# Row mean of 64 MB: a first part of one row per partition in place of sixteen

## The chip, the cores and the metric

The kernel runs on one core of a Trainium2 chip. The metric is the device time of one execution in microseconds (us), given as the median of several runs. The engines that matter here are VectorE (DVE in the profile), ScalarE (ACT), GpSimd (POOL), SyncE (SP, which here only issues DMAs), and the 16 DMA engines that move data between the chip's memory (HBM) and the on-chip memory of 128 partitions (SBUF).

## The reference

```python
def setup_inputs():
    batch, seq, dim = 32, 512, 1024
    return {"x": np.random.randn(batch, seq, dim).astype(np.float32), "divisor": float(dim)}

def reference(x, divisor):
    return (np.sum(x, axis=-1) / divisor).astype(np.float32)
```

There are 32 x 512 = 16,384 rows of 1,024 float32 values, 4 KB a row and 67.1 MB in all. Each row is summed and the sum is divided by 1,024. The result is 64 KB.

## The kernel before

Each of the 128 partitions gets 128 rows (J = 128). The rows are split into three parts, each with its own access pattern into the input.

- The *first* part is F = 16 rows per partition: partition p reads rows 16p to 16p+15 of the first 2,048 rows, so from partition to partition the address goes on by 64 KB. It is read by two loads, of 2 and 14 rows per partition.
- The *main* part is M = 96 rows and the *last* part L = 16 rows per partition. Together they are W = 112 consecutive rows of a partition, so from partition to partition the address goes on by 448 KB. The main part is read by seven loads: five of 14 rows, one of 14 and one of 12.
- The last part is read by loads of 9, 4 and 2 rows, and its sixteenth row in two halves, `pa` and `pb`.

A load of n rows is one DMA of 128 pieces, one per partition, and a piece is n x 4 KB long. All loads are issued from SP in program order (L182), on one queue. The nine loads of the first and main part and the load of 9 rows use a pool of three buffers (`bulk`), 14 rows each. So a load must wait until the reduce of the load three before it has ended. The loads of 4 and 2 rows and the two halves have buffers of their own.

VectorE sums the rows of a bulk load with one instruction (L205). In the last two bulk loads of the main part, ScalarE takes 4 and 5 of the rows (L186); in the lists `first`, `main` and `last` the second number of a pair says how many. POOL multiplies the sums of a part by 1/1024 (L207): `res0` for the first part, `res` for the main part. In the last part, VectorE (L192) and ScalarE sum and scale row by row into `fin`.

Three stores write the result, all from SP: `o_first` (L223) and `o_main` (L224) are placed behind the last loads in program order, `o_last` (L228) stands at the very end. Their pieces are one per partition: 64 B, 384 B and 64 B; in the output, the main and last pieces of neighbouring partitions are 448 B apart.

Three functions change the finished program. `start_loads_at_once` moves the first loads, those without a wait, ahead of the opening barrier; there are three. `latest_wait_first` reorders the waits of an instruction. `close_while_storing` moves the last store into the closing sequence, so that the engines close while it is in flight; POOL there waits for the landings of the first two stores, and SP's last instruction for the landing of the third.

Of the kernel before, what the change touches and what calls it, by code (L numbers as in the profile page):

```python
# [9 lines left out]
F32 = mybir.dt.float32  # L10
# [115 lines left out]
@with_exitstack  # L126
def kernel(
    ctx: ExitStack,
    tc: tile.TileContext,
    x: bass.AP,  # L130
    divisor: float,
    out: bass.AP,
):
    nc = tc.nc
    landed = nc.alloc_semaphore("landed")
    nc.at_finalize(start_loads_at_once)
    nc.at_finalize(latest_wait_first)
    nc.at_finalize(lambda nc: close_while_storing(nc, landed))
    xf = x.flatten_outer_dims()
    N, D = xf.shape  # L140
    P = nc.NUM_PARTITIONS
    scale = 1.0 / float(divisor)
    J = N // P
    assert J * P == N


    F, L = 16, 16
    M = J - F - L
    W = M + L
    x_first = bass.AP(tensor=x.tensor, offset=0, ap=[[F * D, P], [D, F], [1, D]])  # L150
    x_main = bass.AP(tensor=x.tensor, offset=P * F * D, ap=[[W * D, P], [D, M], [1, D]])
    x_last = bass.AP(tensor=x.tensor, offset=P * F * D + M * D, ap=[[W * D, P], [D, L], [1, D]])
    o_first = bass.AP(tensor=out.tensor, offset=0, ap=[[F, P], [1, F]])
    o_main = bass.AP(tensor=out.tensor, offset=P * F, ap=[[W, P], [1, M]])
    o_last = bass.AP(tensor=out.tensor, offset=P * F + M, ap=[[W, P], [1, L]])


    first = [(2, 0), (14, 0)]
    main = [(14, 0)] * 5 + [(14, 4), (12, 5)]
    last = [(9, 4), (4, 2), (2, 1)]  # L160
    assert sum(n for n, _ in first) == F
    assert sum(n for n, _ in main) == M and sum(n for n, _ in last) == L - 1

    pad = ctx.enter_context(tc.tile_pool(name="pad", bufs=1))
    pad.tile([P, 224], F32, name="pad")
    bulk = ctx.enter_context(tc.tile_pool(name="bulk", bufs=3))
    one = ctx.enter_context(tc.tile_pool(name="one", bufs=1))
    psum = ctx.enter_context(tc.tile_pool(name="junk", bufs=4, space=bass.MemoryType.PSUM))


    c = 512
    t4 = one.tile([P, 4, D], F32, name="t4")
    t2 = one.tile([P, 2, D], F32, name="t2")
    pa = one.tile([P, 768], F32, name="pa")[:, :c]
    pb = one.tile([P, D - c + 16], F32, name="pb")[:, : D - c + 2]
    res0 = one.tile([P, F], F32, name="res0")
    res = one.tile([P, M], F32, name="res")
    fin = one.tile([P, L], F32, name="fin")
    nc.gpsimd.memset(pb[:, D - c :], 0.0)  # L179

    def load(dst, src):
        tc.keep_in_program_order(nc.sync.dma_start(out=dst, in_=src))  # L182

    def act_sum(dst, src, by=1.0):
        junk = psum.tile([P, D], F32, name="junk")
        nc.scalar.activation(junk, src, COPY, scale=by, accum_out=dst)  # L186

    def dve_mean(dst, src, by=scale):


        h = src.shape[-1] // 2
        nc.vector.tensor_tensor_reduce(  # L192
            out=src[:, :h], in0=src[:, :h], in1=src[:, h:], scale=by, scalar=0.0,
            op0=ADD, op1=ADD, accum_out=dst,
        )

    for loads, src, dst in ((first, x_first, res0), (main, x_main, res)):
        j = 0
        for rows, on_act in loads:
            t = bulk.tile([P, 14, D], F32, name="t")  # L200
            load(t[:, :rows, :], src[:, j : j + rows, :])
            d = rows - on_act
            for i in range(d, rows):
                act_sum(dst[:, j + i : j + i + 1], t[:, i, :])
            nc.vector.reduce_sum(out=dst[:, j : j + d], in_=t[:, :d, :], axis=AX)  # L205
            j += rows
        nc.gpsimd.tensor_scalar_mul(out=dst, in0=dst, scalar1=scale)  # L207
    j = 0
    for rows, on_act in last:
        t = bulk.tile([P, 14, D], F32, name="t")[:, :rows, :] if rows > 4 else t4 if rows == 4 else t2  # L210
        load(t, x_last[:, j : j + rows, :])
        d = rows - on_act
        for i in range(rows):
            if i < d:
                dve_mean(fin[:, j + i : j + i + 1], t[:, i, :])
            else:
                act_sum(fin[:, j + i : j + i + 1], t[:, i, :], by=scale)
        j += rows
    load(pa, x_last[:, j, :c])
    load(pb[:, : D - c], x_last[:, j, c:])  # L220


    tc.keep_in_program_order(nc.sync.dma_start(out=o_first, in_=res0))  # L223
    tc.keep_in_program_order(nc.sync.dma_start(out=o_main, in_=res))  # L224

    dve_mean(pb[:, D - c : D - c + 1], pa, by=1.0)
    dve_mean(fin[:, j:], pb)
    tc.keep_in_program_order(nc.sync.dma_start(out=o_last, in_=fin))  # L228
# [35 lines left out]
```

## Time and profile before

| | |
|---|---|
| median of 3 runs | 160.81 us (160.39 to 160.96) |
| span of the profiled execution | 159.0 us (the page gives no other time of it; the median is 1.8 us longer) |
| DMA, bytes moved, mean rate | 67.18 MB, 422 GB/s over the span |
| VectorE busy | 117.2 us (74%), of which the bulk reduces 111.2 us |
| ScalarE busy | 18.5 us (12%) |
| POOL busy | 1.0 us (1%) |
| landing of the first load (2 rows) | 4.63 us after the span's start |
| a reduce of 14 rows | 15.09 us |
| last store, issue to landing | 1.4 us |

The span begins with the issue of the first load and ends with the landing of the last store. An engine's share of busy time is an average over the span; what a change in one stage is worth has to be read from that stage, by the wait that ends last there. In the slices of the page each digit is the busy share of a fortieth of the span in tenths. A group's line gives what was waited for, the total of the waits in us, their number, and the longest.

### The profile page before, as it was taken

Reading aid. Unit: us, or ns where it says so; the run is one execution under the profiler, and the core shown is the slowest. Engines: PE = TensorE matmul, PEld = TensorE weight load, DVE = VectorE, ACT = ScalarE, POOL = GpSimd, SP = SyncE. Lnnn points to the kernel's source line nnn. Section 1 sums busy time; section 2 is a strip of 40 time slices with the busy share of each in tenths; the row PEclk is TensorE's granted clock in tenths of the full one; section 3 lists DMA queues with packets and bytes.
Section 4 is the critical chain, followed back from the end, with each engine's and each line's share of the span. In section 5 each row is a group of like instructions: output and inputs, shape, how many; then the busy total and the mean of one; then the engine's idle time right before and its main releaser. Section 6 shows DMA issues by size and latency. Waiting matters only on the chain.

```text
span 159.0 us, 148 instructions
## 1 busy us (share of the span) xinstructions
DVE 117.2 (74%) x29; ACT 18.5 (12%) x33; POOL 1.0 (1%) x7
## 2 busy tenths in 40 slices
DVE  0500059995999599978999599959995996395643
ACT  3000000000000000000000000000000900390684
POOL 0000000000000000000000000000000000001000
DMA  7999999959999999699999999699999999999894
GB/s 278 447 462 462 462 462 462 462 260 433 462 462 462 462 462 462 303 390 462 462 462 462 462 462 404 303 447 462 462 462 429 396 396 408 482 445 445 350 420 169
DMA packets 2448, 67.18 MB, mean 422 GB/s; under 512 B 656, under 2 KB 656, under 8 KB 912
## 3 DMA queue, kind: packets, MB, share of 16 engines
q1 hardware_dynamic: 2448, 67.18, 98.3%
HBM read 67.11 MB, written 0.07 MB: 422 GB/s over the span
## 4 chain that ended last, share of the span: by engine, by line
DMA 77%; DVE 21%; SPq 1%; issue 0%; DVEq 0%
DMA t<-in_x_dram 56%; DMA pb<-in_x_dram 21%; DVE res L205 20%; SPq L182 1%; DVE pb L192 0%; DVEq L259 0%
## 5 line engine op out<-in xcount | busy, mean ns | idle before, releaser
L205 DVE TENSOR_REDUCE res<-t 128x14 f32<-128x14336 f32 (+3 forms) x9 | 111.2, 12360 | 34.0 <-DMA t<-in_x_dram 34.0
L186 ACT ACTIVATE junk<-t 128x1024 f32<-128x1024 f32 x16 | 16.2, 1013 | 136.8 <-DMA t<-in_x_dram 136.8
L192 DVE CUSTOM_DVE_ANT_0 t<-t 128x512 f32<-128x512 f32 x8 | 5.1, 688 | 6.1 <-DMA t<-in_x_dram 6.1
L186 ACT ACTIVATION_READ_ACCUMULATOR junk<-t 128x1 f32 x16 | 3.0, 186 | 0.0
L207 POOL TENSOR_SCALAR res<-res 128x16 f32<-128x16 f32 (+1 forms) x2 | 0.7, 352 | 143.3 <-DVE res L205 143.3
L186 ACT ACT_TABLE_LOAD x1 | 1.3, 1283 | 1.7 <-PEq L245 1.7
L192 DVE DVE_READ_ACCUMULATOR2_ANT fin<- 128x1 f32 x9 | 0.7, 82 | 0.0
L192 DVE CUSTOM_DVE_ANT_0 pb<-pb 128x257 f32<-128x257 f32 x1 | 0.4, 428 | 0.2 <-DMA pb<-in_x_dram 0.2
L192 DVE CUSTOM_DVE_ANT_0 pa<-pa 128x256 f32<-128x256 f32 x1 | 0.4, 426 | 0.0
L179 POOL MEMSET pb<- 128x2 f32 x1 | 0.1, 99 | 1.3 <-POOLq L245 1.3
L245 POOL MEMSET const-bfloat16-1.0<- 128x1 bf16 x1 | 0.1, 101 | 0.0
L245 POOL MEMSET const-uint8-127<- 128x1 uint8 x1 | 0.1, 101 | 0.0
L245 POOL MEMSET const-float32-0.0<- 128x1 f32 x1 | 0.1, 98 | 0.2 <-issue 0.2
L245 POOL MEMSET const-float32-1.0<- 128x1 f32 x1 | 0.1, 98 | 0.0
L192 DVE DVE_READ_ACCUMULATOR2_ANT pb<- 128x1 f32 x1 | 0.1, 84 | 0.0
## 6 DMA issues: line engine op xcount, KB each, us to landing
t<-in_x_dram SPq DMA_DIRECT2D x7, 7168.0 KB, 35.6
t<-in_x_dram SPq DMA_DIRECT2D x1, 6144.0 KB, 33.3
t<-in_x_dram SPq DMA_DIRECT2D x1, 4608.0 KB, 27.2
t<-in_x_dram SPq DMA_DIRECT2D x2, 1024.0 KB, 19.2
t<-in_x_dram SPq DMA_DIRECT2D x1, 2048.0 KB, 31.7
pa<-in_x_dram SPq DMA_DIRECT2D x1, 256.0 KB, 33.8
pb<-in_x_dram SPq DMA_DIRECT2D x1, 256.0 KB, 33.9
out_dram<-res SPq DMA_DIRECT2D x1, 48.0 KB, 11.6
```

The costliest lines, as they stand in the source:

```text
L179: nc.gpsimd.memset(pb[:, D - c :], 0.0)
L182: tc.keep_in_program_order(nc.sync.dma_start(out=dst, in_=src))
L186: nc.scalar.activation(junk, src, COPY, scale=by, accum_out=dst)
L192: nc.vector.tensor_tensor_reduce(out=src[:, :h], in0=src[:, :h], in1=src[:, h:], scale=by, scalar=0.0, op0=ADD, op1=ADD, accum_out=dst,)
L205: nc.vector.reduce_sum(out=dst[:, j : j + d], in_=t[:, :d, :], axis=AX)
L207: nc.gpsimd.tensor_scalar_mul(out=dst, in0=dst, scalar1=scale)
L245: nc = _bacc.Bacc("TRN2", target_bir_lowering=False, num_devices=1)
```

## The change

The first part shrinks from 16 rows per partition to one. Its single load of one row per partition reads 512 KB in one stretch. The main part grows from 96 to 111 rows per partition, and with the 16 rows of the last part each partition now has 127 consecutive rows, so the address goes on by 508 KB from partition to partition. The main part's loads are six of 14 rows, one of 14 and one of 13. The pieces of the three stores are 4 B, 444 B and 64 B, and the main and last pieces of neighbouring partitions are 508 B apart. The tile `res0` keeps its place of 16 values, of which one is used.

```diff
-    F, L = 16, 16
+    F, L = 1, 16
     M = J - F - L
     W = M + L
     x_first = bass.AP(tensor=x.tensor, offset=0, ap=[[F * D, P], [D, F], [1, D]])
...
-    first = [(2, 0), (14, 0)]
-    main = [(14, 0)] * 5 + [(14, 4), (12, 5)]
+    first = [(1, 0)]
+    main = [(14, 0)] * 6 + [(14, 4), (13, 5)]
     last = [(9, 4), (4, 2), (2, 1)]
...
-    res0 = one.tile([P, F], F32, name="res0")
+    res0 = one.tile([P, 16], F32, name="res0")[:, :F]
```

## The prediction

> **What bounds the kernel now.** I read the views in this order: the slices of the page and its table of DMA queues, then the stretches between the landings of the bulk loads, then the chain of the work that ended last, and last the waits of VectorE and of the SP queue. The slices and the queue table:
>
> ```profile
> DVE  0500059995999599978999599959995996395643
> ...
> DMA  7999999959999999699999999699999999999894
> GB/s 278 447 462 462 462 462 462 462 260 433 462 462 462 462 462 462 303 390 462 462 462 462 462 462 404 303 447 462 462 462 429 396 396 408 482 445 445 350 420 169
> ...
> q1 hardware_dynamic: 2448, 67.18, 98.3%
> ```
>
> The sixteen DMA engines are busy 98.3% of the span. The digits 5 and 6 are not holes: a packet of 57,344 B is booked whole in one slice, so its neighbour looks poor. The stretches cut at the landings show that. Columns are the stretch, its length, the busy time of DVE, ACT and POOL, the clock, the DMA share and the rate:
>
> ```profile
> 0.00:4.63 4.63, 0.00 (x0) 1.28 (x1) 0.28 (x5) 1.00 1.10 425
> 4.63:21.51 16.88, 2.29 (x1) 0.00 (x0) 0.00 (x0) 1.00 1.00 435
> 21.51:38.44 16.93, 15.09 (x1) 0.00 (x0) 0.26 (x1) 1.00 1.00 434
> 38.44:55.42 16.98, 15.09 (x2) 0.00 (x0) 0.00 (x0) 1.00 1.00 432
> 55.42:72.33 16.91, 15.09 (x2) 0.00 (x0) 0.00 (x0) 1.00 1.00 434
> ...
> 106.14:123.10 16.96, 15.08 (x1) 0.00 (x0) 0.00 (x0) 1.00 0.98 425
> ...
> 137.65:148.49 10.84, 7.62 (x1) 5.30 (x10) 0.45 (x1) 1.00 0.94 407
> ```
>
> The reader is to see two things. A load of 14 rows lands every 16.88 to 16.98 us at a DMA share of 1.00, so 1.21 us a row, and VectorE needs 15.09 of that. And the pace does not depend on the two spacings that this kernel has: the stretch 4.63:21.51 moves rows 64 KB apart from partition to partition, the later ones rows 448 KB apart, 16.88 against 16.91 to 16.98.
>
> The chain, by engine, and the waits of VectorE and of the SP queue:
>
> ```profile
> DMA 77%; DVE 21%; SPq 1%; issue 0%; DVEq 0%
> ```
> ```profile
> DVE res L205 <- DMA t<-in_x_dram: 34.0, 9, 14.6
> DVE t L192 <- DMA t<-in_x_dram: 6.1, 3, 3.2
> ```
> ```profile
> SPq L182 <- DVE res L205: 92.8, 7, 15.1
> ```
>
> The chain gives VectorE 21%, but only because it follows a load back to the reduce that freed its buffer. With three buffers, load k+3 is issued when the reduce of load k ends, 15.1 us after k landed, when 1.8 us of load k+1 and all of load k+2 are still to come. So SP waits 92.8 us for VectorE at no cost. The time is: issue to first byte, 67.11 MB at the engines' pace, and 1.9 us after the last landing (157.10 to 159.0).
>
> The sum is made against the profiled execution, whose span is 159.0. The runs have a median of 160.81, so 1.8 us lie around the span; I keep those as they are. About 0.5% (0.8 us) is what a measurement here can tell from no change; the three runs alone spread over 0.57 us.
>
> **The change part by part.**
>
> *Loads.* The first part goes from 2 + 14 rows to 1; the main part from five of 14 plus 14 and 12 to six of 14 plus 14 and 13. That is 16 + 96 and 1 + 111: 112 rows both times, in nine loads both times. "One bulk load less" holds for the first part alone; the main part has one more. Each load is 128 pieces, one a partition, so pieces and bytes are the same: 112 rows x 1.21 us on either side, term 0. The first load lands one row earlier, at about 3.4 instead of 4.63, and so does every 14-row load; the 13-row load gives the row back and lands again at 137.65.
>
> *VectorE.* A row costs (15.09 - 2.29) / 12 = 1.07 us. The first reduce takes about 1.2 instead of 2.29, the one of the 13-row load 7.62 + 1.07 = 8.69 (8 rows, ACT still has 5). It ends at 146.3; the next landing is at 148.49, before which VectorE idled 3.2 us and would idle 2.1. Term 0, hidden by the nine-row load. With that cover gone it would cost 1.07.
>
> *Buffers and the SP queue.* Load 4 is issued when the one-row reduce ends, at 3.4 + 1.2 = 4.6 instead of 6.9; until 37.2 the engines have loads 2 and 3. The 13-row load waits for reduce 6 and the nine-row load for reduce 7, each 1.2 us earlier. Behind the nine-row load on SP stand four loads and the first store, 0.33 to 0.48 us of issue each (121.25 to 124.1), while load 9 runs until 137.65. The queue never runs dry. Term 0; the cover is a whole load of 15.7 us.
>
> *POOL.* The scaling of the first result needs only load 1: at 4.6 instead of 36.7. From 16 to 96 columns the operation goes from 0.26 to 0.45 us, 2.4 ns a column, so 111 columns take 0.48. The main store, behind it on SP, is issued at about 146.9 instead of 145.8. In its queue it still stands behind loads that end at 157; nothing on SP is behind it before 157.5. Term 0.
>
> *Start of the load stream.* The first load's pieces shrink from 8 to 4 KB and from 64 KB apart to one stretch of 512 KB. The first piece starts 1.0 us after the issue; the 16 first pieces take 0.31 to 1.01 us against 0.31 later, some 0.5 us of loss on average. The trace shows no load this small at the start. Lower bound: that loss goes, -0.5. Upper: the load runs at half pace, its own 1.2 us once more. Load 2 is issued 0.43 us after load 1, so it is there before 1.2 us of data have passed. I take 0, since the loss is latency of a first piece, whatever its size.
>
> The Trainium skill, "DMA: Bandwidth & Descriptors", section "Measured (HBM→SBUF, 128 partitions, SWDGE, issued from GpSimd)", speaks against this step: it asks for at least 1 MiB a DMA and gives a 1 MB transfer 78% of the peak. By that rule halving the first load would be charged part of its fixed 2 us; the row says otherwise, because loads 2 and 3 stand behind it in the queue.
>
> *Spacing of the rows.* Six full main loads and the 14, 13, 9, 4, 2 and 1 rows are read 508 KB apart instead of 448. No row of the trace has 508. The nearest are 64 and 448 KB: 16.88 against a mean of 16.93, 0.05 us a load, over some nine such lengths 0.5 us either way. An upper bound from the farthest row of full-size loads: the stretch at 425 GB/s against 435, 2.3% of 154 us of transfer, 3.6 us. I take 0, by the nearest rows: a factor of seven in the spacing moved 0.3%.
>
> The Trainium skill, "DMA: Bandwidth & Descriptors", section "Latency and other measured facts", warns of row pitches at large powers of two: copies with a pitch of 512 KiB at 207 GB/s and padded ones at 214. If 508 KB behaved as 512 KB, 207 against 214 would be 3.3%, an estimated 5 us on this page's figures; the page also says that 4 KiB of padding restored the full rate, and 508 KB is 512 less 4. No run here shows a pitch of 512 KB.
>
> *Stores.* The first store shrinks from 64 B a partition to 4 B (128 neighbouring words), the main one grows from 384 to 444 B, and the spacing goes from 448 to 508 B, so that the pieces of the main and last store no longer start at multiples of 64 B. The last store decides: issued at 157.56, 1.4 us to landing, of which its 128 writes take 0.2 and the way from the last write to the landing 0.4. The trace has no store off a 64 B boundary and none of 4 B. Lower bound 0: the first store has less to write but ends before the last is issued. Upper: the way to landing doubles, +1.4. I take +0.1, half of the 0.2 of its writes, because only the edges of the pieces change. The first two stores landed at 157.2 and 157.4; POOL waits for them and closes at 158.2, so they may be 0.7 late for nothing.
>
> Sum: 0 + 0 + 0 + 0 + 0 + 0 + 0.1; span 159.1, time 160.81 + 0.1 = 160.9.
>
> **The rivals.**
>
> A, slower: the reads 508 KB apart meet more often in the memory and the pace of the main loads falls. For it: the pace is the whole kernel, nothing hides it, and this spacing is in no row. Against it: 64 and 448 KB run alike. Price: up to 3.6 us by the row above, 164.5; it decides from 0.8 / 154 = 0.5%, that is, when a 14-row load takes 17.01 instead of 16.92.
>
> B, slower: the unaligned or 4-byte writes land late. For it: the last store lies bare on the path, and so do the other two once they are over 0.7 us late. Against it: writes were hidden or 0.2 us so far. Price up to +1.4: 162.2; it decides from +0.8.
>
> C, faster: the start-up loss of 0.5 goes, and the small slowings in the bulk pieces, which the packet records put at 0.3 us over the whole run. Together -0.8: 160.0, just at the bound. Against it: there is no idle engine to win from anywhere else.
>
> D, the change does not do what it says: no load is saved in total. It changes nothing in the forecast, as no gain was booked for it; it is part of the likeliest case.
>
> **How the numbers follow.** Likeliest case, with D: 0.52, its own range 160.3 to 161.5 (the spread of the runs, -0.5 to +0.7). A gets 0.27 because it multiplies 154 us by an unknown; B 0.13; C 0.08. Slower by over 0.5%: A and B, 0.40. Faster: 0.08. The range starts at 160.2, leaving out half of C (0.04), and runs to 164.9, A's upper bound with the +0.1 of the stores and 0.3 of spread, leaving out about 0.1 of A beyond what a row here bounds.
>
> **What would show it.** In the profile after: the first reduce starts near 3.4 and takes 1.2; 14-row loads land 16.9 us apart at a DMA share of 1.00 and 434 GB/s; the reduce of 8 rows takes 8.7 and ends before 146.5; the last store lands 1.4 to 1.6 us after its issue; the queue's share stays at 98%. Wrong would be: landings 17.1 us apart or more (A); the last landing at 157 as before, but an end beyond 159.8 (B); the last landing below 156.4 (C).

## The result and the profile after

The changed kernel takes 166.38 us (median of 6 runs, 165.9 to 167.2) against 160.84 us before. The ratio is 1.036 with a 95% interval of 1.034 to 1.038: 3.6% or 5.5 us slower. The forecast was 160.9 us, in a range that ended at 164.9. The profiled execution has a span of 164.4 us and took 166.1 us itself, so 1.7 us lie around the span, as before.

The stretches of the changed kernel, cut at the landings of the loads. Columns: the stretch, its length, the busy time of DVE, ACT and POOL, the clock, the DMA share, GB/s.

```profile
0.00:3.43 3.43, 0.00 (x1) 1.28 (x1) 0.28 (x5) 1.00 1.12 420
3.43:20.57 17.14, 1.22 (x2) 0.00 (x0) 0.23 (x1) 1.00 0.99 428
20.57:37.49 16.92, 15.09 (x2) 0.00 (x0) 0.00 (x0) 1.00 1.00 434
37.49:54.40 16.91, 15.08 (x1) 0.00 (x0) 0.00 (x0) 1.00 1.00 434
...
105.13:122.06 16.93, 15.09 (x2) 0.00 (x1) 0.00 (x0) 1.00 0.99 430
...
137.81:148.65 10.84, 8.68 (x1) 5.30 (x10) 0.51 (x1) 1.00 0.97 419
148.65:157.28 8.63, 5.55 (x19) 7.61 (x14) 0.00 (x0) 1.00 0.94 384
157.28:164.40 7.12, 0.43 (x2) 0.00 (x0) 0.00 (x0) 1.00 0.01 1
```

The reader is to see that up to 157.28 nothing has changed. But for the first, which takes 17.14 us, the 14-row loads land 16.9 us apart at 430 to 434 GB/s, as before, although they now read rows 508 KB apart. The last load lands at 157.28 instead of 157.10. Then comes a stretch of 7.12 us, where the kernel before had 1.90 us, and in it the DMA engines move almost nothing: a DMA share of 0.01 and 1 GB/s. So 5.2 of the 5.4 us of longer span lie behind the last load. The slices of the page say the same: the DMA engines are at 9, but for one 6, until the last two slices, which are 2 and 0, and the queue's share of the longer span falls from 98.3% to 95.1%:

```profile
DMA  9999999999999999999999999999999996999920
...
q1 hardware_dynamic: 2448, 67.18, 95.1%
```

What the kernel waits for there is told by the DMA issues, with the KB of each and the time from issue to landing. First the three stores of the kernel before, then those of the changed one:

```profile
out_dram<-res SPq DMA_DIRECT2D x1, 48.0 KB, 11.6
out_dram<-res SPq DMA_DIRECT2D x1, 8.0 KB, 33.6
out_dram<-fin SPq DMA_DIRECT2D x1, 8.0 KB, 1.4
```
```profile
out_dram<-res SPq DMA_DIRECT2D x1, 55.5 KB, 16.4
out_dram<-res SPq DMA_DIRECT2D x1, 0.5 KB, 40.7
out_dram<-fin SPq DMA_DIRECT2D x1, 8.0 KB, 5.9
```

The first store, now 0.5 KB, was issued at 122.60 and lands 40.7 us later, at 163.3; the main store, issued at 147.11, at 163.5; the last store needs 5.9 us in place of 1.4. All three have landed late, and the smallest of them is the first. A store counts up its semaphore in 16 shares. These are the times, in us from the span's start, at which the shares of the three stores arrived in the changed kernel:

```
first  157.03 157.09 157.49 158.62 158.90 160.07 160.09 160.09 160.11 160.12 160.35 160.62 160.95 161.62 161.63 163.29
main   157.21 157.28 158.79 160.26 160.27 160.29 160.52 160.82 160.95 161.78 162.15 162.69 162.98 163.12 163.42 163.47
last   159.00 159.05 159.06 160.43 160.45 160.48 160.69 161.02 161.12 161.94 162.87 163.30 163.30 163.31 163.58 163.64
```

In the kernel before, the shares of the first store arrive within 0.3 us (156.97 to 157.26), those of the main store by 157.43 and those of the last from 158.80 to 158.97. Now they trickle in over 6 us, and the main and last store follow the first. The packet records show the writes of the first and main store as sent by 157.17 and those of the last by 158.77, so it is not the sending that takes the time but what comes behind it. POOL waits for the landings of the first two stores before it closes the kernel, and SP waits for that closing. The waits of the SP queue, first before the change, then after:

```profile
SPq L105 <- SPq L105: 0.8, 1, 0.8
SPq L259 <- PEq L259: 0.2, 1, 0.2
```
```profile
SPq L259 <- PEq L259: 6.1, 2, 5.7
```

L105 is SP's wait for the last store, L259 the closing. In the kernel before, SP ends by waiting for the last store, and the span ends 0.03 us behind its landing. In the changed kernel that wait is gone: when the closing reaches SP, the last store has already landed (163.64). POOL's two waits end at 163.31 and 163.49, with the landings of the first and the main store (163.29 and 163.47), and the closing ends the span at 164.35, 0.88 us behind the main store's landing. So the end of the changed kernel is set by the first two stores through POOL's closing, and the late last store is covered.

### The profile page after: what moved, and what is told of

Same layout as the page of the kernel before. It is cut to its first block, busy times and chain, and to the rows that moved or that the text cites. A ratio compares the mean times of both kernels' runs of the same rounds, so it can differ in the third digit from the quotient of the medians.

```text
span 164.4 us, 148 instructions
## 1 busy us (share of the span) xinstructions
DVE 117.2 (71%) x29; ACT 18.5 (11%) x33; POOL 1.0 (1%) x7
## 3 DMA queue, kind: packets, MB, share of 16 engines
q1 hardware_dynamic: 2448, 67.18, 95.1%
## 4 chain that ended last, share of the span: by engine, by line
DMA 75%; DVE 19%; SPq 1%; issue 0%; DVEq 0%
DMA t<-in_x_dram 54%; DMA pb<-in_x_dram 21%; DVE res L205 19%; SPq L182 1%; DVE pb L192 0%; DVEq L259 0%
## 5 line engine op out<-in xcount | busy, mean ns | idle before, releaser
L207 POOL TENSOR_SCALAR res<-res 128x1 f32<-128x1 f32 (+1 forms) x2 | 0.7, 368 | 144.5 <-DVE res L205 144.5
```

## The experiments

**Theories.** *W*: the 128 neighbouring 4-byte words of the first store are written one after another, and everything behind them on the same DMA engines lands late. *U*: the pieces of the main and last store, 508 B apart and off 64-byte boundaries, are slow. Rival A of the prediction, the reads 508 KB apart, had already fallen with the profile after.

### Without the first store

```diff
-    tc.keep_in_program_order(nc.sync.dma_start(out=o_first, in_=res0))
```

> The changed kernel with the first store left out: the 128 results of the first part are computed but never written. Theory W (the 128 neighbouring 4-byte words of the first store are written one after another, about 52 ns each, from 156.6 to 163.3 us, and everything behind them on the same DMA engines lands late): the last store lands 1.4 to 1.6 us after its issue and the time is that of the kernel before, ratio 1.000, at most 1.003. Theory U (the pieces of the main and last store, 508 bytes apart and off 64-byte boundaries, are what is slow): nothing changes, ratio about 1.035. If both have a share, the ratio lies between and the landing of the last store tells the share of U.

Measured (run e1): 160.6 us, ratio 0.9995 (0.998 to 1.001). The issues of the stores that are left:

```profile
out_dram<-res SPq DMA_DIRECT2D x1, 55.5 KB, 10.4
out_dram<-fin SPq DMA_DIRECT2D x1, 8.0 KB, 1.4
```

The whole loss goes with the first store. The main and last store with their 508-byte spacing cost nothing that can be seen: the last one lands 1.4 us after its issue, as in the kernel before. U falls.

### The kernel before with a first store of 4 bytes per partition

```diff
-    o_first = bass.AP(tensor=out.tensor, offset=0, ap=[[F, P], [1, F]])
+    o_first = bass.AP(tensor=out.tensor, offset=0, ap=[[1, P], [1, 1]])
...
-    tc.keep_in_program_order(nc.sync.dma_start(out=o_first, in_=res0))
+    tc.keep_in_program_order(nc.sync.dma_start(out=o_first, in_=res0[:, :1]))
```

> The kernel before with only its first store changed: it writes one of its 16 columns, 4 bytes per partition to 128 neighbouring words, and leaves the other 15 out. Main and last store keep their 448-byte spacing. Theory W: the loss comes here too, first landings trickle in over 6 to 7 us, ratio about 1.035. Theory U: no loss, ratio 1.000.

Measured (run e2): 166.08 us, ratio 1.034 (1.030 to 1.037).

```profile
out_dram<-res SPq DMA_DIRECT2D x1, 48.0 KB, 17.4
out_dram<-res SPq DMA_DIRECT2D x1, 0.5 KB, 39.3
out_dram<-fin SPq DMA_DIRECT2D x1, 8.0 KB, 5.9
```

So the store alone, put into the kernel before, makes the loss, with 0.5 KB written in place of 8 KB. Nothing of the new reading is needed for it.

### The same words 64 bytes apart

```diff
+    o_first = bass.AP(tensor=out.tensor, offset=0, ap=[[16, P], [1, 1]])
```

Everything else, the store of `res0[:, :1]` too, is as in the run before.

> As the run before, one column of 4 bytes per partition, but each word stays where the kernel before has it, 64 bytes from partition to partition; the other 15 columns are left out. Tells two forms of theory W apart. If the size of a piece is what costs (any write of 4 bytes takes some 50 ns): ratio about 1.035 again. If it is that neighbouring words share a stretch of memory and wait for one another: 64 bytes apart they do not, ratio 1.000 to 1.003. Theory U: 1.000.

Measured (run e3): 160.79 us, ratio 1.0004 (0.999 to 1.002).

```profile
out_dram<-res SPq DMA_DIRECT2D x1, 48.0 KB, 11.6
out_dram<-res SPq DMA_DIRECT2D x1, 0.5 KB, 33.6
out_dram<-fin SPq DMA_DIRECT2D x1, 8.0 KB, 1.4
```

The same 128 writes of 4 bytes are free when they stand 64 bytes apart. It is not the size of a piece but that the pieces are neighbours.

### The first store in the middle of the loads

```diff
             load(t[:, :rows, :], src[:, j : j + rows, :])
+            if dst is res and j == 42:
+                tc.keep_in_program_order(nc.sync.dma_start(out=o_first, in_=res0))
...
-    tc.keep_in_program_order(nc.sync.dma_start(out=o_first, in_=res0))
```

> The changed kernel with the first store moved forward in SP's order, from behind the last load to behind the fifth load, so that its writes fall near 71 us, with some 85 us of loads to follow. Theory W with slow landings alone: the writes trickle in unseen under the loads, the tail is as before the change, ratio 1.000 (160.4 to 161.3 us). Theory W with writes that hold up the loads behind them on the same engines: the 6.5 us, or a part of it, shows as one late landing of a bulk load near 71 to 90 us, and the ratio stays between 1.01 and 1.04. Theory U: ratio about 1.035, with a late landing of the last store.

Measured (run e4): 165.71 us, ratio 1.031 (1.028 to 1.035). The stretches between the landings of four 14-row loads:

```profile
37.41:54.41 17.00, 15.09 (x1) 0.00 (x0) 0.00 (x0) 1.00 1.00 432
54.41:71.45 17.04, 15.09 (x2) 0.00 (x0) 0.00 (x0) 1.00 1.14 431
71.45:93.03 21.58, 15.08 (x1) 0.00 (x0) 0.00 (x0) 1.00 0.88 340
93.03:109.99 16.96, 15.09 (x2) 0.00 (x0) 0.00 (x0) 1.00 1.00 433
```

The last store lands after 1.4 us again, but the load behind the moved store lands 21.58 us after its forerunner instead of 16.9: 4.6 us later. Its packets of 57,344 B take up to 6.9 us instead of 2.1. Reads that stand behind the small writes on the same DMA engines are held up with them, and since the loads are the bound, the delay is carried to the end. The store's own shares trickle in from 71.11 to 76.88 here, as they did at the end. Moving the store does not hide it; of the two forms of W, the one with held-up loads is the right one.

### All rows 512 KB apart

```diff
-    x_main = bass.AP(tensor=x.tensor, offset=P * F * D, ap=[[W * D, P], [D, M], [1, D]])
+    x_main = bass.AP(tensor=x.tensor, offset=F * D, ap=[[J * D, P], [D, M], [1, D]])
...
-    o_first = bass.AP(tensor=out.tensor, offset=0, ap=[[F, P], [1, F]])
+    o_first = bass.AP(tensor=out.tensor, offset=0, ap=[[J, P], [1, F]])
```

The other four patterns go the same way.

> The changed kernel with each partition given 128 consecutive rows: all parts are read 512 KB apart, and the first store's 4-byte words stand 512 bytes apart. Theory W: no neighbouring words any more, so the tail is that of the kernel before; what is left is the pace of the reads. By the rows of the kernels so far (16.9 us for a 14-row load at 64, 448 and 508 KB): 16.9 us, ratio 1.000 to 1.003. If reads a power of two apart do meet in the memory, which was rival A in its strongest form: 14-row loads at 17.1 us or more, ratio 1.01 to 1.035, all of it in the loads and none behind the last landing.

Measured (run e5): 161.02 us, ratio 1.001 (0.999 to 1.003).

```profile
20.82:37.73 16.91, 15.09 (x1) 0.00 (x0) 0.00 (x0) 1.00 1.00 434
37.73:54.71 16.98, 15.09 (x1) 0.00 (x0) 0.00 (x0) 1.00 1.00 432
54.71:71.61 16.90, 15.09 (x1) 0.00 (x0) 0.00 (x0) 1.00 1.00 434
```

But for the load behind the short first one, 17.38 us here and 17.14 in the changed kernel, rows 512 KB apart are read at the same pace as rows 64, 448 and 508 KB apart. And the 4-byte words, now 512 B apart, cost nothing. So with one row per partition in the first part, and without neighbouring words, the time is that of the kernel before.

### How close is too close

Eight forms of the first store in the kernel before. The lags and spans are those of one profiled execution each, on several chips. All but the form of the kernel before leave out the columns that they do not write. The lag is from the last landing of the last load to the last landing of the main store, which stands right behind the first on the DMA engines. Each row changes the access pattern of `o_first` (`[[2, P], [1, 2]]` and so on) and the number of columns.

Run e6:

> The kernel before with its first store writing 8 of the 16 columns, 32 bytes per partition and 32 bytes apart; the other 8 are left out. 128 neighbouring pieces as with 4 bytes, but two to a 64-byte block instead of 16. If the price is one wait for each further piece in a 64-byte block (5.9 us for 15, 0.39 us each): the first store's last landing is 0.6 us behind that of the last load, against 0.2 in the kernel before, span 159.0 to 159.4. If the block is 32 bytes: 0.2 us, span 159.0. If any 128 neighbouring pieces below 64 bytes cost 46 ns each: 6 us behind, span about 164.

Run e7:

> As e6 with 4 columns, 16 bytes per partition and 16 bytes apart, four to a 64-byte block; the other 12 are left out. By one wait for each further piece in a 64-byte block: 3 x 0.39 + 0.2 = 1.4 us behind the last load, span about 159.7. In blocks of 32 bytes (0.82 us a further piece): 1.0 us, span about 159.4. By 46 ns a piece: 6 us, span about 164.

Run e8:

> As e6 with 2 columns, 8 bytes per partition and 8 bytes apart, eight to a 64-byte block; the other 14 are left out. By one wait for each further piece in a 64-byte block: 7 x 0.39 + 0.2 = 2.9 us behind the last load, span about 161.2. In blocks of 32 bytes: 3 x 0.82 + 0.2 = 2.7 us, span about 161. By 46 ns a piece: 6 us, span about 164.

Run e10:

> The kernel before with its first store writing one column, 4 bytes per partition, 32 bytes apart; the other 15 columns are left out. Blocks of 32 bytes: each word alone, nothing lost, the first two stores land 0.2 and 0.35 us behind the last load, span 159.0 to 159.4. Blocks of 64 bytes: two to a block, the stores land some 0.4 to 0.8 us later than that.

Run e11:

> As e10 with the words 16 bytes apart: two to a 32-byte block, as with the pieces of 16 bytes in e7, whose main store landed 1.35 us behind the last load. Theory block with 32 bytes: the same 1.0 to 1.4 us, whatever the size of a piece. If the bytes written mattered: less than in e7. If nothing is lost, the loss of e7 was that of 16-byte pieces and not of sharing a block.

| first store, 128 pieces | run | stretch written | lag, us | span, us |
|---|---|---|---|---|
| 64 B, 64 B apart (kernel before) | before | 8 KB | 0.35 | 159.0 |
| 32 B, 32 B apart | e6 | 4 KB | 0.33 | 159.1 |
| 16 B, 16 B apart | e7 | 2 KB | 1.35 | 159.6 |
| 8 B, 8 B apart | e8 | 1 KB | 2.56 | 160.7 |
| 4 B, 4 B apart | e2 | 512 B | 6.19 | 164.3 |
| 4 B, 16 B apart | e11 | 2 KB | 0.94 | 159.4 |
| 4 B, 32 B apart | e10 | 4 KB | 0.72 | 159.2 |
| 4 B, 64 B apart | e3 | 8 KB | 0.33 | 159.2 |

For pieces that touch, the loss sets in between 32 and 16 bytes and more than doubles with each halving: 1.0, 2.2 and 5.8 us beyond the 0.35 of the kernel before. Single words lose a little even at 32 bytes apart (e10, 0.4 us). The loss follows the distance far more than the bytes: 8 bytes at 8 apart lag 2.56, while 4 bytes at 4, 16 and 64 apart lag 6.19, 0.94 and 0.33. The lags around 1 us should not be ranked among themselves: the first store's own last share lands 0.30, 0.42 and 0.55 us behind the last load in e7, e11 and e10, the reverse of the order of the main store. Pieces of 32 bytes are free though two of them share 64 bytes, so one wait of 0.39 us for each further piece in a 64-byte block, one of the forms expected, is not right. About 1 us of lag stays unseen, since the kernel has the last sum, the issue of the last store and its 1.4 us to go through in that time; e10 and e11 show it, with spans of 159.2 and 159.4 that end 0.03 us behind the last store. In e2, e7 and e8, as in the changed kernel, the span ends 0.88 us behind the main store instead: there POOL's closing sets the end.

### Blocks or stretch

Two forms of W fit this table: the number of writes that share a small block, or the number that fall in a short stretch of memory. In the table both change together, so the next four stores are to part them: 4-byte words in groups, all from `res0[:, :1]`.

```diff
+    o_first = bass.AP(tensor=out.tensor, offset=0, ap=[[128, 16], [1, 8], [1, 1]])   # e9
+    o_first = bass.AP(tensor=out.tensor, offset=0, ap=[[8, 16], [1, 8], [1, 1]])     # e13
+    o_first = bass.AP(tensor=out.tensor, offset=0, ap=[[1, 16], [128, 8], [1, 1]])   # e14
+    o_first = bass.AP(tensor=out.tensor, offset=0, ap=[[16, 16], [1, 8], [1, 1]])    # e15
```

Run e9:

> The kernel before with its first store writing one column, 4 bytes per partition, in 16 groups of 8 neighbouring words, the groups 512 bytes apart; the other 15 columns are left out. So the words share 32-byte blocks as fully as in e2, but are spread over 8 KB as in e3. Theory block (writes below 32 bytes into the same 32-byte block wait for one another, about 0.8 us for each further one): 7 x 0.8, so the stores land some 5 to 6 us behind the last load, span about 164. Theory region (it is the short stretch of memory, 512 bytes in all, that holds the 128 writes up, whichever block they are in): 8 KB is harmless, span 159.0 to 159.4. With blocks of 64 bytes and 0.39 us each: 2.9 us, span about 161.

Run e13:

> As e9, the same 16 groups of 8 neighbouring words, but the groups stand next to one another, so that the 128 words fill the same 512 bytes as in e2. Only the distance of the groups differs from e9, and only the order in which the transfer is described from e2. If the short stretch counts: 5 to 6 us behind the last load as in e2, span about 164. If e9 was cheap because its transfer is described in groups: below 1 us as in e9, span 159.0 to 159.4.

Run e14:

> As e9 with 8 groups of 16 neighbouring words, 64 bytes a group and 512 bytes from group to group, and the words of a group from partitions that stand 8 apart. Every 64-byte block is as full as in e2, the blocks are as far apart as in e9. If how many writes share a block decides: 5 to 6 us behind the last load, span about 164. If the length of the stretch decides: about 1 us as in e9, span 159.0 to 159.5.

Run e15:

> As e13 with the groups of 8 words 64 bytes apart, 1 KB in all: eight writes to a 64-byte block, as in e8, where the main store landed 2.6 us behind the last load. If the length of the stretch or the number in a block decides: 2 to 3 us, span 159.7 to 161. If the groups decide: below 1 us.

| words | run | in 512 B | lag, us | span, us |
|---|---|---|---|---|
| 16 groups of 8, 512 B apart | e9 | 8 | 0.95 | 159.2 |
| 8 groups of 16, 512 B apart | e14 | 16 | 1.61 | 159.9 |
| 16 groups of 8, 64 B apart | e15 | 64 | 2.50 | 161.7 |
| 16 groups of 8, side by side | e13 | 128 | 5.80 | 164.0 |

The span of e15 includes 1.0 us of later landing of its last load (158.32), which the store, standing behind that load in the queue, cannot have caused; the lag leaves that out. e13 came out as the same transfer as e2 (in both traces a destination of 128 by 1 pieces, where e9, e14 and e15 have 16 by 8), so it repeats e2 (5.80 against 6.19) and says nothing on the order in which a transfer is described. e15 does: it was described in groups and lags 2.50, like the plain 8-byte pieces of e8 (2.56), which also fill 1 KB.

Neither form holds alone. Full groups of 16 words spread 512 B apart (e14) lag 1.61, not 6, so sharing a block does not make the loss by itself. But e9 has as few words in 512 B as e3 has and lags 0.95 where e3 has 0.33, so neighbours in a group do count. The groups also differ in how the partitions are dealt out to them, and the traces do not tell which DMA engine writes which word, so a share of the engines in this is not ruled out. What the runs give is a rule of thumb: beyond the 0.35 of the undisturbed kernel, 128 writes in one stretch of 512 B cost 5.5 to 5.9 us, 64 in each cost 2.2, 32 cost 0.6 to 1.0, and 16 or 8 cost 0 to 1.3, mostly the more the closer they stand. 5.9 us, the loss in the changed kernel (6.22 less 0.35), over 128 writes are 46 ns each. Why, inside the memory or on the way to it, no run here shows; that stays open.

### The words gathered into one row first

```diff
+    row = one.tile([1, P], F32, name="row")
...
             load(t[:, :rows, :], src[:, j : j + rows, :])
+            if dst is res and j == 42:
+                tc.keep_in_program_order(nc.sync.dma_start(out=row, in_=res0))
...
-    tc.keep_in_program_order(nc.sync.dma_start(out=o_first, in_=res0))
+    tc.keep_in_program_order(nc.sync.dma_start(out=o_first, in_=row))
```

Here `o_first` is one piece of 512 bytes.

> The changed kernel with a detour: behind the fifth load the 128 results of the first part are copied by a DMA from one value per partition to 512 bytes in one partition of the on-chip memory, and the first store at the end writes these 512 bytes in one stretch. Theory W, block or region: no small neighbouring writes to HBM are left, ratio 1.000 to 1.004. If 128 neighbouring 4-byte writes are as slow on chip as in HBM, the copy holds up the loads near 71 us as in e4, ratio about 1.03.

Measured (run e12): 160.86 us, ratio 1.001 (0.9995 to 1.002). The reduces of the loads around the copy, each of which starts when its load has landed:

```profile
54.37 15.09 DVE L208 TENSOR_REDUCE res<-t 128x14 f32<-128x14336 f32 x1 [1.82 <-DMA t<-in_x_dram]
71.85 15.09 DVE L208 TENSOR_REDUCE res<-t 128x14 f32<-128x14336 f32 x1 [2.39 <-DMA t<-in_x_dram]
88.76 15.09 DVE L208 TENSOR_REDUCE res<-t 128x14 f32<-128x14336 f32 x1 [1.83 <-DMA t<-in_x_dram]
```

The copy writes the same 128 neighbouring words, but on chip, and lands at 72.02, 0.2 us behind the load in front of it (71.83). That load lands 17.48 us after its forerunner, 0.6 us more than the usual 16.9; behind it the loads are 16.9 us apart again, where e4 had one of 21.58. By the interval of the ratio at most 0.4 us of it is left in the time. So the loss belongs to neighbouring small writes into HBM. This repairs the changed kernel; it does not beat the one before, and no form here does, because both are bound by the same loads.

## Why the prediction was wrong

- *Loads, VectorE, buffers, SP, POOL: right.* First landing 3.43 (forecast 3.4), first reduce 1.22 (1.2), the other 14-row loads 16.90 to 16.93 apart (16.9), reduce of 8 rows 8.69 and its end at 146.5 (8.7, 146.3), main store issued at 147.11 (146.9), last load landed at 157.28 (157.1). One 14-row load, the first, took 17.14; it belongs to the next step.
- *Start of the load stream: right within what can be told.* Term 0: the last landing moved by 0.18 us in all. The load behind the short one landed at 20.57, where 21.51 less one row of 1.21 gives 20.30; its 17.14 us pass the 17.1 that was named as the sign of rival A, but they come from the start, as the later loads show. So the 512-KB load at the head of the queue cost 0.3 us there, and nothing that can be told from the spread at the end. The Trainium skill's advice of at least 1 MiB a DMA ("DMA: Bandwidth & Descriptors", section "Measured (HBM→SBUF, 128 partitions, SWDGE, issued from GpSimd)") does not bear on one load among others in a full queue, and the trace of this case decides that way.
- *Spacing of the rows: right*, for 508 KB and, by e5 with its ratio of 1.001, for 512 KB too, so the 5 us that were estimated for that case did not come either. Rival A got the second largest chance, 0.27, for a price that was never paid. Its 3.6 us rested on a row misread: the stretch at 425 GB/s is 16.96 us long like the others (16.88 to 16.98), so its load was no slower, and the GB/s of a stretch depends on which side of its ends whole packets are booked.
- *Stores: wrong, and this is the step that failed.* The forecast was +0.1, bounded by +1.4. Behind the last landing the profile has +5.2, and the run without the first store gives the whole of it back. Two parts of the step were wrong. First, the path: it said "the last store decides" and gave the first a lower bound of 0 because it "has less to write". The runs showed that this store, one sixteenth of its former bytes, decides: POOL's closing waits for it and for the main store behind it, and the span ends 0.88 us after the main store's landing. The last store is late too (5.9 us in place of 1.4), behind the first, but it does not set the end. Second, the cost: the upper bound took one way to landing, 1.4 us, once. The rows were those of pieces that stand 64 B apart, and none bounds writes that stand side by side: 128 of these cost 5.9 us together, 46 ns for each, and no row of the kernel before has that price, so the bound should have been left open.
- *Rival B* had the right place and both signs of it (last landing where it was, end beyond 159.8), with a price of 1.4 us where 5.2 was measured; so its chance of 0.13 stood for a case whose true time lay outside the range. The slack of 0.7 us that the step gave POOL's wait was right (0.69 us: in the kernel before, the main store lands 1.57 us ahead of the end, and the closing takes 0.88), and the first store came 6.0 us later (163.29 against 157.26).
- *Rival D* was right and without effect.

## What to carry to other kernels

When a layout is changed for the reads, look at what it does to the writes: a partition that keeps one row of results writes 4 bytes, and 128 such words side by side cost 5.5 us here, while 64-byte pieces, 32-byte pieces or words 64 bytes apart cost nothing. Do not count on hiding such a store under the loads of a kernel that is bound by them, since loads behind it on the same DMA engines wait with it; keep 32 bytes or more per partition, or gather the words into one row on chip first. And where no row of the trace bounds an operation, call its price open, and multiply a doubtful price by the number of pieces before calling it small.

## What the runs showed of the hardware

- 128 writes of 4 bytes to 512 neighbouring bytes of HBM take 5.5 to 5.9 us longer to be confirmed (e13, e2 and the changed kernel; 46 ns each for 5.9), though the packet records show them as sent by 157.17, before the last load's landing is reported at 157.25; the same words 64 bytes apart (e3), or the same 512 bytes in one piece (e12), take nothing that can be seen. The Trainium skill, "DMA: Bandwidth & Descriptors", section "Specifications", names 512 bytes as the least size for the full rate and a read-modify-write below it. That bears on size alone, and here size alone was free: 4-byte pieces 64 bytes apart gave a ratio of 1.0004. Whether a read-modify-write takes place, no run here shows.
- A store that is confirmed late delays what stands behind it on the same DMA engines: the main and last store at the end (163.47 and 163.64 behind 163.29), and in the run with the early store a bulk read, whose packets took up to 6.9 us instead of 2.1.
- The same writes into the on-chip memory (e12) delayed the load beside them by 0.6 us and the whole by at most 0.4 us.
- Full-size loads whose rows stand 64, 448, 508 and 512 KB apart from partition to partition landed 16.87 to 16.98 us apart in the kernel before, the changed one and e5; only the load behind the short first one took longer (17.14 in the changed kernel, 17.38 in e5).
